# A mixture-of-experts stage on one core: where a place's sums are halved, when its result is added, and how short chunks are turned

## The chip, the cores and the metric

The kernel runs on one core of a Trainium2 chip. The metric is the device time of one execution in microseconds. It computes a two-layer trunk on 256 context and 256 latent tokens of width 1024, all in fp32. The change concerns the last stage of the second layer, the experts, which takes from about 900 us to the end.

## The reference, cut to what matters

```
def swiglu(h, wg, wu, wd):
    return (jax.nn.silu(h @ wg) * (h @ wu)) @ wd

def moe_ffn(h, w_r, wg, wu, wd):          # h: 256 x 1024, 8 experts, hidden width 2816
    logits = (h @ w_r).astype(jnp.float32)
    top_v, top_i = lax.top_k(logits, 2)
    gates = jax.nn.softmax(top_v, axis=-1)
    combine = jnp.sum(jax.nn.one_hot(top_i, 8) * gates[..., None], axis=-2)
    out = jnp.zeros_like(h)
    for e in range(8):
        out = out + combine[..., e:e + 1] * swiglu(h, wg[e], wu[e], wd[e])
    return out
# in the last layer: x = x + mod[5] * moe_ffn(...)
```

## The kernel before

After routing, the eight experts are put in order of their token counts into eight places (expert 0 is always place 7). A place has a fixed number of slots, `CAPS`: 160, 128, 128, 64, 64, 64, 32, 32. Places 0, 1 and 2 are wide: 128 slots, their weights split into a high and a low fp32r half (`whi` by a ScalarE copy, `wlo` by a VectorE subtraction, lines 275 and 276) and multiplied in three products. Place 0's slots beyond 128 are a 32-slot rest, called `NE`, which uses place 0's weights again. The 64- and 32-slot places multiply plain fp32, with several column blocks of a weight side by side in the array (`tiled`, `tiled_up`).

An expert's hidden width is cut into 11 chunks of 256. A chunk needs three loads of 1 MB: two for gate and up (`gu`), one for down (`dn`). `rounds()` sets the order: 4 rounds with a chunk of place 7 each, then 11 rounds each for places 1, 0 and 2, with one chunk of a 64-slot place (3, then 4, then 5) in each and a 32-slot chunk (places 7 and 6) in 6, 6 and 4 of them, then two rounds with a chunk of place 6. A round of `experts()` (line 1605) does: the wide chunk's gate products; the down product of the wide chunk of the round before (`down`, accumulating in two banks `py` over the 11 chunks); for place 0 the rest's gate (`gux`) and down (`down_rest`, `pyx`); the 32-slot and then the 64-slot chunk's gate and the down products of the round before (`down_small`, accumulating in the one bank `pys` or `pyx` of that slot count). Then the round's results are turned, so that the hidden width lies on the partitions: `turn` for the narrow ones, side by side in one bank `mTx`, and two transposes into a bank `mT` for the wide one. A 32-slot chunk lies in two parities on the partitions, which are added: `turn` multiplies it with `sel`, the sum of an identity and a swapped identity, so that one product turns and adds. `split` makes `mh` and `ml` of the wide chunk, `turned` makes silu(gate) times up (`silx`) of the narrow ones (line 1584). `mT`, `mTx`, `ohT`, `sc` and others share two banks.

When a place's last down product is issued, `finishes(p)` starts a chain (line 1747). Finishes go one after the other, whatever the place: each waits for the flag `finishing`. `finish` (line 1754) waits for the place's transposed one-hot matrix `ohT` (made by `onehot`, at most two at a time), multiplies the sums by the modulation row (`y`, lines 1766 and 1770), splits `y` into `yh` and `yl`, waits 3.0 us of the planner's clock, and then, per block of columns and half of the tokens, multiplies with `ohT` (a pair of `sc` products) and adds the gated result into `acc` (line 1780). A wide place does this in two halves of 512 columns, the second `y` made after the first half's pairs. The last place to finish stores `acc` block by block; that is place 6.

The order on TensorE and ScalarE in this stage is the order in which the program issues the instructions (`MSB = "pa"`); VectorE's and the load queue's order is chosen by the framework. The main order is `experts()`; chains like `finish`, `onehot` and `gather` are woven in at each of its `yield`s when the planner's clock `o.clk` has reached their due time. The clock advances by an estimated cost per product and, at `Weights.get`, to the modelled landing or split of a weight. All loads go through 12 raw buffers on one queue (SP).

```
RUNS = ((None, (4, 0)), (1, (6, 11)), (0, (6, 11)), (2, (4, 11)), (None, (2, 0)))
SMALL = ((7, 6), (3, 4, 5))
```

Of the kernel before, what the change touches and what calls it, by code (L numbers as in the profile page):

```python
# [18 lines left out]
P = 128  # L19
D = 1024  # L20
KB = D // P
# [4 lines left out]
NE = 8  # L26
# [3 lines left out]
EPS = 1e-6  # L30
# [179 lines left out]
def until(cond):  # L210
    while not cond():
        yield 0.5
# [128 lines left out]
class Net:  # L341
# [1150 lines left out]
    def onehot(self, p):  # L1492

        nc = self.nc
        yield from until(lambda: len(self.ohT) < 2)
        self.ohT[p] = None
        oh = self.mp.tile([P, 2, P], F32, tag="oh1", name="oh1", bufs=1)
        n = self.slots(p)
        for t in range(2):
            nc.vector.tensor_scalar(oh[:, t, :].rearrange("p (a b) -> p a b", b=n), self.c("iota", 0, n).unsqueeze(1).to_broadcast([P, P // n, n]),  # L1500
                                    self.pos0[:, t, 0:1] if p == NE - 1 else self.pos[:, t, p:p + 1], None, op0=ALU.is_equal)
        yield 1.5
        pt = self.bank("ohT")
        for t in range(2):
            self.tp(pt[:, P * t:P * t + P], oh[:, t, :])
        ohT = self.mp.tile([P, 2, P], F32R, tag="ohT", name="ohT", bufs=2)
# [5 lines left out]
    YB, YH = 1, 1  # L1512
    NRAW, MKRAW = 4, 5
    MPRAW, HL_B, LAG, NS = 3, 2, 6.0, 2
    PIECE, LANDS, SPLIT = 2.45, 4.8, 1.15
# [57 lines left out]
        self.nc.scalar.activation(v, ps[:, :256], AF.Copy)  # L1573
        return v

    def turn(self, pt, at, v, m):
        for j in range(2):
            b = v[:, P * j:P * j + P]
            if m == 32:
                self.mm(pt[:, at + 64 * j:at + 64 * j + 64], b, self.sel, True, True)  # L1580
            else:
                self.tp(pt[:, at + P * j:at + P * j + P], b)

    def turned(self, pt, at, m):

        src = pt[:, at:at + 4 * m].rearrange("p (j g s) -> p j g s", j=2, g=2)
        s = self.mp.tile([P, 2, m], F32, tag=f"silx{m}", name="silx", bufs=5 if m == 32 else 4)
        self.act_fn(s, src[:, :, 0, :], AF.Silu)
        self.nc.vector.tensor_tensor(s, s, src[:, :, 1, :], op=ALU.mult)
        return s  # L1590

    def experts(self):
# [8 lines left out]
        self.sel = self.mp.tile([P, 64], F32, name="sel", bufs=1)  # L1601
        nc.vector.tensor_tensor(self.sel, self.c("ident", 0, 64), self.c("swap", 0, 64), op=ALU.add)
        o.spawn(self.gather(0), 2)
        pw, pn = None, []
        for w, ns in self.rounds() + [(None, [])]:
# [5 lines left out]
            if w:  # L1611
                p, c = w
                x = self.xe[p]
# [39 lines left out]
            mids = []  # L1653
# [37 lines left out]
            at = 0  # L1691
            for p, c, m, v in mids:
                mx = self.turned(pt, at, m)
                at += 4 * m
                if p == NE:
                    pw[4] = mx
                else:
                    pn.append((p, c, mx))
            yield

    def down(self, p, c, mh, ml):
        a, z = c == 0, c == NCH - 1
        if a:
            self.py[p] = [self.pp.tile([P, 512], F32, tag="py", name="py", bufs=2) for _ in range(2)]
        w = self.w.get(("dn", p, c))
        for j in range(2):
            js = slice(P * j, P * j + P)
            for i, (u, v) in enumerate(((mh, w[0]), (ml, w[0]), (mh, w[1]))):
                for n in range(2):
                    ws = slice(D * j + 512 * n, D * j + 512 * n + 512)  # L1710
                    self.mm(self.py[p][n], u[:, js], v[:, ws], a and j == 0 and i == 0, z and j == 1 and i == 2)
        if c == NCH - 2 and p:
            self.o.spawn(self.onehot(p), 1)
        if z and p:
            self.o.spawn(self.finishes(p), 1)
        return w

    def down_rest(self, w, c, mx):
# [11 lines left out]
            self.o.spawn(self.onehot(0), 1)  # L1730
            self.o.spawn(self.onehot(NE), 1)
        if c == NCH - 1:
            self.o.spawn(self.finishes(0), 1)

    def down_small(self, p, c, mx):
        if c == 0:
# [5 lines left out]
        if c == NCH - 2:  # L1742
            self.o.spawn(self.onehot(p), 1)
        if c == NCH - 1:
            self.o.spawn(self.finishes(p), 1)

    def finishes(self, p):
        yield from until(lambda: not self.finishing)
        self.finishing = True
        for q in (p, NE) if p == 0 else (p,):  # L1750
            yield from self.finish(q)
        self.finishing = False

    def finish(self, p):

        nc = self.nc
        m = self.slots(p)
        parts = P // m
        w = 512 if m > 32 else 256
        yield from until(lambda: self.ohT.get(p) is not None)  # L1760
        ohT = self.ohT[p]
        for n in range(2 if m == P else 1):
            yh, yl = (self.mp.tile([P, 512], F32R, tag=nm, name=nm, bufs=self.YH) for nm in ("yh", "yl"))
# [9 lines left out]
            for g in (n,) if m == P else range(parts):  # L1773
                cs = slice(w * g, w * g + w)
                rows = slice(m * g, m * g + m) if parts > 1 else slice(0, P)
                for t in range(2):
                    pz = self.bank("sc")
                    for i, v in enumerate((yh, yl)):
                        self.mm(pz[:, :w], ohT[rows, t, :], v[rows, :w], i == 0, i == 1)
                    nc.vector.scalar_tensor_tensor(self.acc[:, t, cs], pz[:, :w], self.gate[:, t, p:p + 1], self.acc[:, t, cs],  # L1780
                                                   op0=ALU.mult, op1=ALU.add)
                    if self.ndone == NE:
                        nc.sync.dma_start(self.out[P * t:P * t + P, cs], self.acc[:, t, cs])
                    yield 1.0
        del self.ohT[p]
        self.ndone += 1

    def overflow(self):

# [85 lines left out]
    def run(self):  # L1875
# [7 lines left out]
        with tc.tile_pool(name="keep", bufs=1) as keep, ExitStack() as self.pools, ExitStack() as self.kax, tc.tile_pool(name="sm", bufs=2) as self.sp, \  # L1883
                tc.tile_pool(name="w", bufs=2) as self.wp:
            self.const = keep.tile([P, NKEEP], F32, name="const")
            self.params = keep.tile([P, NPARAM], F32, name="params")
            self.csil = keep.tile([P, KB, 38], F32, name="csil")
            self.eps = keep.tile([P, 1], F32, name="eps")
            self.modT = [keep.tile([P, 48, 2], F32, name=f"modT{l}") for l in range(2)]
            self.wr = keep.tile([P, KB, NE], F32, name="wr")  # L1890
            self.acoef = keep.tile([P, 16], F32, name="acoef")
            self.nsink = keep.tile([P, 16], F32, name="nsink")
            nc.scalar.dma_start(self.csil, d["cT"])
            self.act_fn(self.csil, self.csil, AF.Silu)
            nc.scalar.dma_start(self.params, d["params"])
            nc.scalar.dma_start(self.const[:, :2 * P], d["consts"][:, :2 * P])
            nc.vector.memset(self.eps, EPS)
            self.act_fn(self.acoef, self.par("a_log"), AF.Exp)
            nc.vector.tensor_scalar(self.acoef, self.acoef, -1.0, None, op0=ALU.mult)
            nc.vector.tensor_scalar(self.nsink, self.par("sink"), -1.0, None, op0=ALU.mult)  # L1900
            self.nb, self.nc_banks = 4, 3
            self.w = Weights(self, self.plan(), self.nraw, self.nhi)
            with tc.tile_pool(name="psA", bufs=4, space=PSUM) as self.pp, tc.tile_pool(name="g", bufs=self.ng) as self.gp:
                self.ka = self.kax.enter_context(tc.tile_pool(name="keepA", bufs=1))
                self.gb = self.kax.enter_context(tc.tile_pool(name="act", bufs=2 * KB))
                self.xpp = self.kax.enter_context(tc.tile_pool(name="xp", bufs=2))
                self.xT = [self.G(name=f"xT{k}") for k in range(KB)]
# [37 lines left out]
```

## Time and profile before

| | |
|---|---|
| three timed runs | 1581.52, 1585.33, 1587.26 us (median 1585.33) |
| the profiled execution | 1583.83 us; its span on the core 1582.1 us; granted TensorE clock 0.978 |
| TensorE busy | 1500.2 us (95%) |
| VectorE, ScalarE, GpSimd busy | 821.2, 666.7, 102.6 us |
| HBM read | 393.47 MB, of it 264 expert loads of 1 MB |

A row of the profile is a group of instructions with its busy time, or, in a timeline, one instruction or a run of like ones with its start and duration; in brackets stands how long the engine sat idle before it and what released it. PE is TensorE's products, PEld its weight loads, DVE VectorE, ACT ScalarE. A DMA share near 1 means that the 16 DMA engines moved packets all the time. A matmul's record overlaps its neighbours, so the spacing of starts, not the duration, is the price of one in a stream.

### The profile page before, as it was taken

How to read it: one execution, taken by the hardware profiler on the slowest of the kernel's cores; microseconds unless marked ns; L12 is line 12 of the kernel's file. 1: busy time of each engine (PE TensorE's matmuls, PEld its weight loads, DVE VectorE, ACT ScalarE, POOL GpSimd, SP SyncE). 2: the span in 40 equal slices, each digit the busy share in tenths (PEclk: the TensorE clock that was granted, in tenths of full speed). 3: DMA queues.
4: the chain of work that ended last, by engine and by line, in shares of the span. 5: the costliest groups of instructions: out<-in, count | busy, mean ns of one | idle time of the engine just before them, and what ended most of it. 6: DMA issues, size and time to landing. Idle time of an engine off the chain costs nothing. (4 is left out here: it accounts for less than half of the span.)

```text
span 1582.1 us, 23498 instructions
## 1 busy us (share of the span) xinstructions
PE 1500.2 (95%) x9302; PEld 1081.1 (68%) x9303; DVE 821.2 (52%) x1481; ACT 666.7 (42%) x1189; POOL 102.6 (6%) x135
## 2 busy tenths in 40 slices
PE   5999998899999999999999899999999999999997
PEld 1766675787887787878757776666566666656654
DVE  2687568543232333378774344544465444654545
ACT  3566644443222312266455354444343443433441
POOL 1200123210000000030300000000000000000000
PEclk9999999999999999999999899999999999999998
DMA  9422055333323323333164499999998999999994
GB/s 372 152 106 107 28 211 202 133 133 112 129 91 149 133 107 113 112 141 142 56 267 181 152 418 419 419 419 420 418 390 358 371 413 417 419 402 407 419 420 158
DMA packets 57715, 396.10 MB, mean 250 GB/s; under 512 B 6528, under 2 KB 8576, under 8 KB 10496
## 3 DMA queue, kind: packets, MB, share of 16 engines
q1 hardware_dynamic: 56016, 392.03, 62.2%
q10 hardware_dynamic: 1584, 2.52, 0.4%
q8 instruction: 75, 1.23, 0.3%
q14 instruction: 40, 0.33, 0.1%
HBM read 393.47 MB, written 1.05 MB: 249 GB/s over the span
## 5 line engine op out<-in xcount | busy, mean ns | idle before, releaser
L276 DVE TENSOR_TENSOR wlo<-wraw,whi 128x1024 fp32r<-128x1024 f32 (+2 forms) x318 | 377.0, 1222 | 161.2 <-ACT whi L275 155.9
L275 ACT ACTIVATE whi<-wraw 128x1024 fp32r<-128x1024 f32 (+2 forms) x318 | 320.0, 1047 | 148.5 <-PE fd L374 57.9
L374 PE MATMUL gu<-whi,xw 128*128 128x512 f32 x528 | 169.1, 401 | 4.2 <-ACT whi L275 4.2
L374 PE MATMUL gu<-wraw,xs 128*64 128x256 f32 (+1 forms) x1760 | 166.2, 386 | 0.5 <-ACT xs L1484 0.5
L374 PEld LDWEIGHTS gu<-wraw,xs 128*64 128x64 f32 (+1 forms) x1760 | 94.4, 127 | 64.3 <-issue 14.6
L374 PEld LDWEIGHTS gu<-whi,xw 128*128 128x128 f32 x528 | 96.9, 190 | 24.5 <-ACT whi L275 6.1
L374 PE MATMUL gu<-wlo,xw 128*128 128x512 f32 x264 | 104.9, 397 | 3.5 <-DVE wlo L276 3.5
L1162 DVE TENSOR_TENSOR fsil<-fsil,fu 128x512 f32<-128x512 f32 x22 | 15.1, 688 | 153.5 <-PE fu L374 118.2
L374 PE MATMUL pys<-wraw,silx 128*32 128x256 f32 (+1 forms) x616 | 87.6, 480 | 6.8 <-DVE y L1770 4.1
L425 ACT ACTIVATE fsil<-fg 128x512 f32<-128x512 f32 x22 | 13.1, 598 | 174.3 <-PE fg L374 174.3
L1573 ACT ACTIVATE mid<-gu 128x256 f32<-128x256 f32 x55 | 21.0, 382 | 137.1 <-PE gu L374 137.1
L374 PE MATMUL fg<-ahi,whi 128*128 128x512 f32 (+1 forms) x192 | 72.3, 377 | 0.0
L374 PE MATMUL fg<-alo,whi 128*128 128x512 f32 (+1 forms) x192 | 71.6, 373 | 0.2 <-POOL alo L523 0.2
L374 PE MATMUL fg<-ahi,wlo 128*128 128x512 f32 (+1 forms) x192 | 71.4, 372 | 0.0
L374 PE MATMUL fu<-alo,whi 128*128 128x512 f32 (+1 forms) x192 | 71.4, 372 | 0.0
L374 PE MATMUL fu<-ahi,wlo 128*128 128x512 f32 (+1 forms) x192 | 71.3, 372 | 0.0
L374 PE MATMUL fu<-ahi,whi 128*128 128x512 f32 (+1 forms) x192 | 71.3, 372 | 0.0
L374 PE MATMUL fd<-mhi,whi 128*128 128x512 f32 (+1 forms) x188 | 70.7, 376 | 0.0
L374 PE MATMUL fd<-mlo,whi 128*128 128x512 f32 (+1 forms) x188 | 70.6, 375 | 0.0
L374 PE MATMUL fd<-mhi,wlo 128*128 128x512 f32 (+1 forms) x188 | 70.6, 375 | 0.0
L374 PE MATMUL modp<-wraw,csil 128*32 128x512 f32 x384 | 56.7, 628 | 12.0 <-ACT csil L425 6.9
L374 PEld LDWEIGHTS gu<-wlo,xw 128*128 128x128 f32 x264 | 49.9, 189 | 18.3 <-DVE wlo L276 7.4
(342 smaller groups left out, 2831.8 us busy)
## 6 DMA issues: line engine op xcount, KB each, us to landing
wraw<-in_moe_dram SPq DMA_DIRECT2D x264, 1024.0 KB, 12.6
wraw<-in_wmod_dram SPq DMA_DIRECT2D x48, 1024.0 KB, 6.4
wraw<-in_fgu_dram SPq DMA_DIRECT2D x22, 1024.0 KB, 4.8
wraw<-in_win_dram SPq DMA_DIRECT2D x16, 1024.0 KB, 4.9
wraw<-in_wout_dram SPq DMA_DIRECT2D x8, 1024.0 KB, 6.2
wraw<-in_fdn_dram SPq DMA_DIRECT2D x8, 1024.0 KB, 6.2
wraw<-in_fdn_dram SPq DMA_DIRECT2D x4, 768.0 KB, 4.9
wraw<-in_wgd_dram SPq DMA_DIRECT2D x2, 1056.0 KB, 4.9
```

Of the source, the lines that this page charges most:

```text
L275: nc.scalar.activation(hi[:, cs], t[:, cs], AF.Copy)
L276: nc.vector.tensor_tensor(lo[:, cs], t[:, cs], hi[:, cs].bitcast(F32), op=ALU.subtract)
L374: self.nc.tensor.matmul(out, l, r, start=start, stop=stop)
L425: self.last_act = self.nc.scalar.activation(out, in_, func, **kw)
L1162: self.nc.vector.tensor_tensor(s, s, pu, op=ALU.mult)
L1573: self.nc.scalar.activation(v, ps[:, :256], AF.Copy)
```

## The change

A place's `y`, `yh` and `yl` are made by a new function `halves`, which `finished` runs at once when the place's last down product has been issued. A wide place's four halves of 512 columns lie in a buffer of the gathered tokens (`xw`). The chain that is left, `finish`, waits 3.0 us from there, or from the end of the modelled splits, and does the pairs. There is a flag for wide and one for narrow places, so one finish of either kind can be under way; a third `ohT` buffer is added. The finish of `NE` follows place 0's as a narrow one. The place that stores is named (`self.last`, place 6), and its pairs wait until all others are issued.

`turn` transposes every chunk plainly. A turned 32-slot chunk has 256 columns; `turned` copies the first parity of each half to SBUF on ScalarE and adds the second on VectorE (`sum32`) before silu and multiplication. The wide chunk is turned as the last of the round's jobs, and two jobs share a bank. Constants that only the first phase reads move from the pool `keep` into that phase's pool.

```diff
 def onehot(self, p):
-        yield from until(lambda: len(self.ohT) < 2)
+        yield from until(lambda: len(self.ohT) < 3)
...
-    def turn(self, pt, at, v, m):
+    def turn(self, pt, at, v):
         for j in range(2):
-            b = v[:, P * j:P * j + P]
-            if m == 32:
-                self.mm(pt[:, at + 64 * j:at + 64 * j + 64], b, self.sel, True, True)
-            else:
-                self.tp(pt[:, at + P * j:at + P * j + P], b)
+            self.tp(pt[:, at + P * j:at + P * j + P], v[:, P * j:P * j + P])
 
     def turned(self, pt, at, m):
-        src = pt[:, at:at + 4 * m].rearrange("p (j g s) -> p j g s", j=2, g=2)
+        src = pt[:, at:at + 256]
+        if m == 32:
+            v = src.rearrange("p (j r c) -> p j r c", j=2, r=2)
+            src = self.mp.tile([P, 2, 64], F32, tag="sum32", name="sum32", bufs=2)
+            self.nc.scalar.activation(src, v[:, :, 0, :], AF.Copy)
+            self.nc.vector.tensor_tensor(src, src, v[:, :, 1, :], op=ALU.add)
+            src = src.rearrange("p j (g s) -> p j g s", g=2)
+        else:
+            src = src.rearrange("p (j g s) -> p j g s", j=2, g=2)
...
-            if mids:
-                pt, at = self.bank("mTx"), 0
-                for *_, m, v in mids:
-                    self.turn(pt, at, v, m)
-                    at += 4 * m
+            jobs = [[x, x[3]] for x in mids] + ([[None, sil]] if w else [])
+            for i, x in enumerate(jobs):
+                if i % 2 == 0:
+                    pt = self.bank("mT" if i + 1 == len(jobs) else "mTx")
+                self.turn(pt, 256 * (i % 2), x[1])
+                x[1] = pt
             pw = None
             if w:
-                pm = self.bank("mT")
-                for j in range(2):
-                    self.tp(pm[:, P * j:P * j + P], sil[:, P * j:P * j + P])
+                at = 256 * ((len(jobs) - 1) % 2)
...
-                self.split(mh, ml, pm[:, :256])
+                self.split(mh, ml, jobs[-1][1][:, at:at + 256])
...
-    def finishes(self, p):
-        yield from until(lambda: not self.finishing)
-        self.finishing = True
-        for q in (p, NE) if p == 0 else (p,):
-            yield from self.finish(q)
-        self.finishing = False
...
+    def halves(self, p):
...
+        if m == P:
+            f = self.mp.tile([P, 2, KB, P], F32R, tag="xw", name="fin", bufs=2).rearrange("p a k s -> p (a k s)")
+            ys = [(f[:, 1024 * n:1024 * n + 512], f[:, 1024 * n + 512:1024 * n + 1024]) for n in range(2)]
+        else:
+            ys = [tuple(self.mp.tile([P, 512], F32R, tag=nm, name=nm, bufs=1) for nm in ("yh", "yl"))]
+        for n, (yh, yl) in enumerate(ys):
             y = self.mp.tile([P, 512], F32, tag="xsum", name="y", bufs=self.YB)
...
             self.split(yh[:, :w], yl[:, :w], y[:, :w])
-            yield 3.0
...
+        return ys
+
+    def finishes(self, p):
+        yield from self.finish(p, self.begin(p))
+        if p == 0:
+            yield from until(lambda: not self.finishing[False])
+            yield from self.finish(NE, self.begin(NE))
+
+    def begin(self, p):
+        self.finishing[self.wide(p)] = True
+        return self.halves(p)
+
+    def finished(self, p):
+        self.o.wait(lambda: not self.finishing[self.wide(p)])
+        self.o.spawn(self.finishes(p), 1)
+        self.o.poll()
+
+    def finish(self, p, ys):
...
+        yield max(3.0, self.w.splits - self.o.clk + 3.0)
+        yield from until(lambda: self.ohT.get(p) is not None)
+        ohT = self.ohT[p]
+        if p == self.last:
+            yield from until(lambda: self.ndone == NE)
...
```

## Rows read from the trace of the kernel before

**Rows 1.** Stretches: from:to and length, busy us (instructions) by engine, TensorE clock, DMA share, GB/s.

```profile
910.00:1150.00 240.00, 228.90 (x1560) 153.42 (x1553) 114.43 (x151) 109.93 (x182) 0.00 (x0) 0.99 1.01 419
1150.00:1300.00 150.00, 148.84 (x1192) 99.07 (x1190) 74.97 (x107) 62.99 (x107) 0.00 (x0) 1.00 0.94 381
1370.00:1460.00 90.00, 85.63 (x504) 55.41 (x506) 51.78 (x71) 34.74 (x53) 0.00 (x0) 0.96 1.00 406
```

**Rows 2.** Weight loads issued from 1100 to 1120, then from 1540: issue to landing.

```profile
DMA to landing us min/median/max: 19.8/19.8/19.9
...
L240 SPq DMA_DIRECT2D wraw<-in_moe_dram x1: 337/337/337, 1540.3 to 1540.3; - x1
DMA to landing us min/median/max: 16.3/16.3/16.3
```

**Rows 3.** Timeline of the tail: start, us, instruction, count, idle before and releaser.

```profile
1561.05 1.07 PE L374 MATMUL pys<-wraw,silx 128*32 128x256 f32 x16 [0.67 <-DVE silx L1589]
...
1569.00 1.29 DVE L1770 TENSOR_TENSOR y<-pys,mod5row 32x256 f32<-32x256 f32 x3
...
1570.41 0.42 ACT L437 ACTIVATE yh<-y 128x256 fp32r<-128x256 f32 x1 [5.92 <-DVE y L1770]
...
1570.88 0.57 PE L374 MATMUL sc<-yh,ohT 32*128 32x256 f32 x1 [2.68 <-ACT yh L437]
```

**Rows 4.** Timeline, turns at the end of a round of place 0.

```profile
1167.30 1.10 PE L374 MATMUL mTx<-sel,mid 128*128 128x64 f32 x8
...
1168.24 0.39 PE L379 MATMUL mTx<-const,mid 128*128 128x128 f32 x2
...
1168.46 0.38 PE L379 MATMUL mT<-const,sil 128*128 128x128 f32 x2
```

**Rows 5.** Groups of the expert phase: shapes, count, busy us, mean ns, idle before.

```profile
L374 PE MATMUL mTx<-sel,mid 128*128 128x64 f32 x132 | 20.2, 283 | 0.5 <-ACT mid L1573 0.5
...
L1780 DVE SCALAR_TENSOR_TENSOR acc<-sc,gate,acc 128x512 f32<-128x512 f32 x24 | 17.8, 750 | 28.0 <-PE sc L374 27.7
...
L1589 DVE TENSOR_TENSOR silx<-silx,mTx 128x128 f32<-128x128 f32 x33 | 9.3, 282 | 6.9 <-ACT silx L425 6.9
...
L425 ACT ACTIVATE silx<-mTx 128x128 f32<-128x128 f32 x33 | 9.1, 275 | 11.8 <-DVE silx L1589 11.8
...
L437 ACT ACTIVATE yh<-y 128x512 fp32r<-128x512 f32 x9 | 5.6, 625 | 9.1 <-DVE y L1766 5.4 <-PE sc L374 3.7
...
L1766 DVE TENSOR_TENSOR y<-py,mod5row 128x512 f32<-128x512 f32 x6 | 4.2, 692 | 4.1 <-PE py L374 3.9
```

**Rows 6.** Timeline, ScalarE and VectorE after the turns of two rounds.

```profile
1169.88 0.22 ACT L425 ACTIVATE silx<-mTx 128x64 f32<-128x64 f32 x1 [0.50 <-DVE silx L1589]
...
1171.47 2.01 ACT L275 ACTIVATE whi<-wraw 128x1024 fp32r<-128x1024 f32 x2 [0.80 <-PE gu L374]
...
1369.47 0.38 ACT L437 ACTIVATE mh<-mT 128x256 fp32r<-128x256 f32 x1 [3.13 <-PE mT L379]
...
1372.26 0.41 DVE L438 TENSOR_TENSOR ml<-mT,mh 128x256 fp32r<-128x256 f32 x1
```

**Rows 7.** Timeline around the first products of place 5, then two stretches.

```profile
1365.55 1.94 PE L374 MATMUL pys<-wraw,silx 128*64 128x512 f32 x8
...
1381.05 1.95 PE L374 MATMUL gu<-wraw,xs 128*64 128x256 f32 x16
...
1386.37 0.69 DVE L1770 TENSOR_TENSOR y<-pys,mod5row 64x512 f32<-64x512 f32 x1
...
1387.12 3.68 PE L374 MATMUL pys<-wraw,silx 128*64 128x512 f32 x8 [4.12 <-DVE y L1770]
...
1390.73 0.69 PE L379 MATMUL mTx<-const,mid 128*128 128x128 f32 x2
...
1380.00:1390.00 10.00, 5.88 (x32) 2.13 (x26) 5.86 (x7) 1.75 (x3) 0.00 (x0) 0.77 1.01 419
1390.00:1400.00 10.00, 10.00 (x41) 7.30 (x40) 4.91 (x10) 4.16 (x7) 0.00 (x0) 0.89 1.01 418
```

More of the change, by code (lines that the diff above doesn't have):

```diff
@@ L1511 @@
     SU = 4.0
-    YB, YH = 1, 1
+    YB = 1
     NRAW, MKRAW = 4, 5
@@ L1598, in experts @@
         self.xe, self.ohT, self.py = {}, {}, {}
-        self.finishing = False
+        self.finishing = [False, False]
         self.ndone = 0
-        self.sel = self.mp.tile([P, 64], F32, name="sel", bufs=1)
-        nc.vector.tensor_tensor(self.sel, self.c("ident", 0, 64), self.c("swap", 0, 64), op=ALU.add)
+        self.last = self.steps()[-1][1]
         o.spawn(self.gather(0), 2)
@@ L1714, in down @@
         if z and p:
-            self.o.spawn(self.finishes(p), 1)
+            self.finished(p)
         return w
@@ L1732, in down_rest @@
         if c == NCH - 1:
-            self.o.spawn(self.finishes(0), 1)
+            self.finished(0)
     def down_small(self, p, c, mx):
@@ L1744, in down_small @@
         if c == NCH - 1:
-            self.o.spawn(self.finishes(p), 1)
-    def finishes(self, p):
-        yield from until(lambda: not self.finishing)
-        self.finishing = True
-        for q in (p, NE) if p == 0 else (p,):
-            yield from self.finish(q)
[L1752 to L1757, printed above, removed]
+            self.finished(p)
+    def halves(self, p):
+        nc, m = self.nc, self.slots(p)
         parts = P // m
         w = 512 if m > 32 else 256
[L1760 to L1763, printed above, removed]
+        if m == P:
[4 more added lines that the diff above has]
+        for n, (yh, yl) in enumerate(ys):
             y = self.mp.tile([P, 512], F32, tag="xsum", name="y", bufs=self.YB)
@@ L1771, in finish @@
             self.split(yh[:, :w], yl[:, :w], y[:, :w])
-            yield 3.0
[L1773 to L1784, printed above, removed]
+        return ys
@@ new lines, in finishes @@
+    def finishes(self, p):
[11 more added lines that the diff above has]
+    def finish(self, p, ys):
+        nc = self.nc
+        m = self.slots(p)
+        parts = P // m
+        w = 512 if m > 32 else 256
+        wide = m == P
+        yield max(3.0, self.w.splits - self.o.clk + 3.0)
[3 more added lines that the diff above has]
+            yield from until(lambda: self.ndone == NE)
+        for g in range(D // w):
+            cs = slice(w * g, w * g + w)
+            rows = slice(0, P) if wide else slice(m * g, m * g + m)
+            for t in range(2):
+                pz = self.bank("sc")
+                for i, v in enumerate(ys[g if wide else 0]):
+                    self.mm(pz[:, :w], ohT[rows, t, :], v[rows, :w], i == 0, i == 1)
+                nc.vector.scalar_tensor_tensor(self.acc[:, t, cs], pz[:, :w], self.gate[:, t, p:p + 1], self.acc[:, t, cs],
+                                               op0=ALU.mult, op1=ALU.add)
+                if p == self.last:
+                    nc.sync.dma_start(self.out[P * t:P * t + P, cs], self.acc[:, t, cs])
+                yield 1.0
@@ L1785, in finish @@
         del self.ohT[p]
         self.ndone += 1
+        self.finishing[wide] = False
     def overflow(self):
@@ L1886, in run @@
             self.params = keep.tile([P, NPARAM], F32, name="params")
-            self.csil = keep.tile([P, KB, 38], F32, name="csil")
             self.eps = keep.tile([P, 1], F32, name="eps")
-            self.modT = [keep.tile([P, 48, 2], F32, name=f"modT{l}") for l in range(2)]
+            self.modT = [None, keep.tile([P, 48, 2], F32, name="modT1")]
             self.wr = keep.tile([P, KB, NE], F32, name="wr")
[L1891 to L1900, printed above, removed]
             self.nb, self.nc_banks = 4, 3
@@ L1904, in run @@
                 self.ka = self.kax.enter_context(tc.tile_pool(name="keepA", bufs=1))
+                self.csil = self.ka.tile([P, KB, 38], F32, name="csil")
+                self.modT[0] = self.ka.tile([P, 48, 2], F32, name="modT0")
+                self.acoef = self.ka.tile([P, 16], F32, name="acoef")
+                self.nsink = self.ka.tile([P, 16], F32, name="nsink")
+                nc.scalar.dma_start(self.csil, d["cT"])
+                self.act_fn(self.csil, self.csil, AF.Silu)
+                nc.scalar.dma_start(self.params, d["params"])
+                nc.scalar.dma_start(self.const[:, :2 * P], d["consts"][:, :2 * P])
+                nc.vector.memset(self.eps, EPS)
+                self.act_fn(self.acoef, self.par("a_log"), AF.Exp)
+                nc.vector.tensor_scalar(self.acoef, self.acoef, -1.0, None, op0=ALU.mult)
+                nc.vector.tensor_scalar(self.nsink, self.par("sink"), -1.0, None, op0=ALU.mult)
                 self.gb = self.kax.enter_context(tc.tile_pool(name="act", bufs=2 * KB))
```

11 lines of the change are left out of this document (6 added, 5 removed).

## The prediction

> **What bounds the kernel now.** I read the stretches of the expert phase first [rows 1]. From 910 to 1150 us the DMA engines move 419 GB/s at a share of 1.01: transfers set the pace there. From 1150 to 1300 they move 381 GB/s while TensorE is busy 148.84 of 150 us; these are the rounds of place 0. From 1370 to 1460 they move 406 GB/s. Against 419 the two later stretches lose 150 x (1 - 381/419) = 13.6 us and 90 x (1 - 406/419) = 2.8 us of transfer time. All expert weights pass through 12 raw buffers, so the transfers pause where TensorE is late in freeing them.
>
> The time from issue to landing [rows 2] says how near TensorE is to the transfers. At 1100 to 1120 it is 19.8 us, about eight pieces of 2.5 us (1.05 MB at 419 GB/s) queued ahead: TensorE uses what lands. The last piece is issued at 1540.3 and lands 16.3 us later, at 1556.6; its product, the last `pys` [rows 3], starts at 1561.05. So at the end TensorE lies 4.4 us behind the transfers, and from about 1150 on it is TensorE's own order of work that carries the time, with the transfers close beneath. The end then has a tail: from the end of that `pys` at 1562.1 to the end of the span at 1582.1.
>
> **Part 1: 32-slot chunks turned plainly.** Before, two chunks are turned by eight matmul records with the `sel` matrix, from 1167.30 to 1168.24, 0.47 us a chunk; the plain turn of a 64-slot chunk, two records, takes from 1168.24 to 1168.46, 0.22 us [rows 4]. After, each 32-slot chunk costs the plain price: 0.25 us less on TensorE. 132 records [rows 5] at four a chunk are 33 chunks: 22 of places 7 and 6 and 11 of the rest `NE`. Place 0's rounds hold 6 + 11 of them, place 2's hold 4: 17 x 0.25 = 4.3 us and 4 x 0.25 = 1.0 us. The 10 chunks ahead of place 0's rounds lie where transfers set the pace and are worth nothing; two of the last rounds belong to the tail.
>
> In exchange each chunk gets a ScalarE copy and a VectorE add of 128x128. The nearest rows are the `silx` steps of that shape that read the same bank: 0.275 and 0.282 us [rows 5]; I take these, with nothing and twice that as ends. 17 x 0.56 = 9.5 us of busy time on two engines that are busy 63 and 75 of the 150 us [rows 1], so beside TensorE's products. On ScalarE's order little is added: today the second `silx` of a bank waits 0.50 us for VectorE's multiply out of it [rows 6]; after, the multiply reads SBUF, and the add takes that wait's place. The first reader of the turned chunk is the next round's down product, behind a whole wide gate product.
>
> **Part 2: halves at the last down product.** A 64-slot place's sums lie in a bank of which there is one. Place 4's were read by `y` only behind the finishes of place 0 and of `NE`, the second half at 1386.37; place 5's first down product waited for it 4.12 us on TensorE [rows 7]. Behind that wait the granted clock is 0.77 and 0.89 in two windows of 10 us [rows 7], part of the time at 1.2 instead of 2.4 GHz: the eight `pys` records take 3.68 us against 1.94 at full clock, 1.74 us more. The turns behind them (0.69 against 0.39 for the same two records [rows 4, 7]) and the first gate products run at the low level too; an estimate of 0.6 us from these rows. Together 6.4 us. After, `y` follows the last down product at once, a whole round ahead of the next place's, so this wait goes; what is late next there is the landing of the weights.
>
> The halves cost what they cost before: for a wide place two `y` of 0.69, two `yh` of 0.63 us and two `yl`, taken like `y` [rows 5]. What is new is their place in ScalarE's order, which is fixed with TensorE's: ScalarE stands at `yh` until the product and `y` have ended, and the copies of `mid` and the splits (`whi`) behind it wait. One buffer for `y` makes a wide place's six steps a chain of about 4 us. The narrow products that follow last longer than this (a 64-slot gate takes two groups of 1.95 us and its down product 1.94 [rows 7]), and the next split weights are wanted a round later, so I count nothing; without that cover up to 4 us for each of the two wide places with wide rounds behind them.
>
> **Part 3: finishes side by side, the tail.** Today, after the last `pys`, TensorE and VectorE still do two pairs of place 2 and all four of place 5, then place 6's `y` (three of four parts at 1569.00), `yh` at 1570.41, and place 6's first pair at 1570.88 [rows 3]: 8.8 us after 1562.1. After, places 2 and 5 finish in turn from the narrow rounds on; by the planner's clock (3.0 from the halves, 1.0 between pairs) half of their eight pairs stand ahead of that `pys` and about four behind. Behind it then come four adds into `acc` of 0.75 us [rows 5], four `y` of 0.43, one `yh` of 0.42 [rows 3] and some 0.7 us of gaps: 3.0 + 1.7 + 0.4 + 0.7 = 5.8, so 3.0 us less. The last chunk's turn is on the path: -0.25 for the plain turn, +0.56 for copy and add and 0.1 for two hand-overs, 0.4 us later. Tail: -2.6 us. With all pairs still behind it is 0, with none -6.0. Place 6's own eight pairs and the stores are untouched.
>
> **Part 4: the rest.** Constants that only the first phase reads move to its pool, `sel` goes, and a third one-hot buffer comes. No engine's order in the first phase changes by this; other addresses can make a load wait for another tile. I count nothing, and a microsecond either way.
>
> **Sum.** TensorE's path: 4.3 + 1.0 + 6.4 = 11.7 us. The transfers cap it: of 13.6 us lost, 4.3 return in place 0's rounds, the 2.8 us go, and of the 4.4 us between last landing and last product some 3.4 can be caught up: 10.5 us. I take 9.5, one microsecond for new small waits. With the tail 12.1 us. The profiled execution took 1583.83 us (span 1582.1 and 1.7 around it): 1571.7. Its time is 1.5 us below the median of the runs, 1585.33; from that it is 1573.2. I say 1573.
>
> **Rivals.** *The transfers keep the time.* Only the 2.8 us of the later stretch return and the tail's 2.6, because the additions on ScalarE eat what TensorE saves in place 0's rounds: 5 us, 1580. For it: TensorE is only 4.4 us behind the landings at the end. Against: the transfers, not TensorE, have the gaps [rows 1].
>
> *ScalarE stands behind VectorE.* In 18 of the 33 wide rounds (those with an even number of turned chunks: 5 of place 1, 6 of place 0, 7 of place 2) the wide chunk and the 64-slot chunk now share a bank; before they never did. Two readers of one bank come one after the other here, as the 0.50 us show [rows 6]. So ScalarE's `silx` of the 64-slot chunk will wait for VectorE's `ml`, and `ml` can stand behind splits: `mh` ended at 1369.85 and `ml` began only at 1372.26, 2.4 us later [rows 6]. The next `whi` waits behind it; it had 0.80 us to spare [rows 6]. So up to 1.6 us late in a round, in the 13 rounds of places 0 and 2: 21 us, against 12 gained: +9, 1593. It decides from about 0.9 us a round on. Against it: other `ml` follow `mh` quickly, and the gate products ahead give more cover than that 0.80.
> The Trainium skill, PSUM — Partial Sum Buffer, section on bank collisions, says the same more strictly: no two engines may touch one bank in the same quadrant at once, ScalarE and VectorE reading included, and the compiler puts a dependency between them. By that rule the sharing costs in every such round. The trace agrees that the wait is there; that it reaches TensorE, no row shows.
>
> *The tail does not shorten.* VectorE has to fit eight adds of 0.75 us, the halves and the new adds into the last 12 us; then the sum is 9.5 alone, 1576, still on the forecast's side.
>
> **Chances.** Forecast, the tail's rival included: 0.66. Transfers keep the time: 0.22. ScalarE behind VectorE: 0.09. Something small either way, as loads moved by addresses: 0.03. About 0.5%, 7.9 us, is what a measurement can tell from no change. So faster by more (under 1577.4) 0.66, within it 0.24, slower 0.10. The range: the tail at its best and the full 11.7 give 17.7 us, 1567.6, and 2 us below that for waits that I don't see, 1565.5; upward it takes in the first rival and no change, 1585. The forecast's own range is 1566 to 1577.
>
> **What would show it.** Right: no wait of `pys` for `y` and a clock of 1.00 near 1380; the transfers from 1150 to 1300 above 381 GB/s; two records a turned 32-slot chunk; place 6's first `sc` pair some 6 us after the last `pys`. Wrong: ScalarE idle in front of `silx` with VectorE's `ml` as releaser and TensorE's wide products waiting for `whi` behind it; `yh` holding ScalarE through a wide gate product; or the transfers from 1150 to 1300 at 381 GB/s again.

## The result, and the profile after

The changed kernel takes 1592.49 us (median of 16 runs, 1587.36 to 1595.54) against 1583.39 (16 runs, 1579.17 to 1587.40): 1.0055 times as long, 95% interval 1.0042 to 1.0067. It is slower by 9.1 us, outside the forecast's range. The profiled execution has a span of 1590.9 us against 1582.1 and a granted clock of 0.972 against 0.978; TensorE is busy 1501.1 us, VectorE 830.7, ScalarE 674.7.

Where the span grew, by events that both traces have:

| | before | after | |
|---|---|---|---|
| last norm of the first phase starts (`rs_v`, line 403) | 889.3 | 895.0 | +5.7 |
| first down product of place 1 starts (`py`) | 945.4 | 952.5 | +7.1 |
| transfer time lost, 1120 to 1300: 180 x (1 - rate/419) | 387 GB/s: 13.7 | 373 GB/s: 19.8 | +6.1 |
| the same, 1380 to 1460: 80 x (1 - rate/419) | 404 GB/s: 2.9 | 419 GB/s: 0 | -2.9 |
| last weight lands | 1556.6 | 1567.1 | +10.5 |
| end | 1582.1 | 1590.9 | +8.8 |

In what follows the start of that norm stands for the end of the first phase. 7.1 + 6.1 - 2.9 = 10.3 of the 10.5 us. The transfers of the expert phase set the end in both kernels; they begin later, lose more around place 0, and only the later loss is gone. The stretches of the changed kernel, in the columns of [rows 1] (from:to, length, busy us by engine, clock, DMA share, GB/s):

```profile
910.00:1150.00 240.00, 226.20 (x1586) 148.91 (x1580) 110.65 (x154) 112.86 (x193) 0.00 (x0) 0.98 1.00 415
1150.00:1300.00 150.00, 143.21 (x1142) 94.56 (x1138) 80.04 (x118) 62.63 (x112) 0.00 (x0) 0.98 0.89 363
1370.00:1460.00 90.00, 86.38 (x509) 53.91 (x508) 55.94 (x75) 38.36 (x57) 0.00 (x0) 1.00 1.01 419
1380.00:1390.00 10.00, 7.34 (x29) 4.61 (x27) 9.86 (x14) 4.41 (x8) 0.00 (x0) 1.00 1.01 419
1390.00:1400.00 10.00, 10.00 (x57) 5.78 (x58) 5.18 (x9) 4.19 (x5) 0.00 (x0) 1.00 1.01 419
```

Against [rows 1, 7]: from 1370 on the loss is gone and the clock at 1380 to 1400 is 1.00, as forecast. From 1150 to 1300 the rate is 363, lower than the 381 before, and TensorE, which was busy nearly all of it, is idle for 6.8 us. TensorE's waits of the expert phase (waiting product, releaser, total us, times, longest) name the place:

```profile
PE gu L374 <- DVE wlo L276: 6.5, 15, 0.9
PE sc L374 <- DVE ml L438: 5.5, 1, 5.5
PE gu L374 <- ACT whi L275: 5.5, 4, 2.6
PE pys L374 <- DVE silx L1593: 4.5, 3, 2.8
```

The wait of `pys` for `y` (4.12 us in [rows 7]) is not among them; one wait of 5.5 us for `ml` is new. In the timeline (start, us, instruction, count, idle before and releaser) it stands at the end of place 1:

```profile
1152.90 0.63 PE L379 MATMUL mTx<-const,mid 128*128 128x128 f32 x4 [0.94 <-DVE acc L1806]
1153.36 0.38 PE L379 MATMUL mT<-const,sil 128*128 128x128 f32 x2
...
1153.51 4.63 DVE L276 TENSOR_TENSOR wlo<-wraw,whi 128x1024 fp32r<-128x1024 f32 x4
...
1158.77 0.42 DVE L438 TENSOR_TENSOR ml<-mT,mh 128x256 fp32r<-128x256 f32 x1
...
1159.25 1.22 PE L374 MATMUL sc<-fin,ohT 128*128 128x512 f32 x2 [5.51 <-DVE ml L438]
1160.27 1.05 PE L374 MATMUL gu<-whi,xw 128*128 128x512 f32 x2
...
1159.42 0.26 ACT L425 ACTIVATE silx<-sum 128x64 f32<-128x64 f32 x1 [4.84 <-DVE sum L1587]
...
1164.88 2.01 ACT L275 ACTIVATE whi<-wraw 128x1024 fp32r<-128x1024 f32 x2 [5.03 <-issue]
```

Both shared banks are full of turned chunks. A finish product (`sc`) stands next in TensorE's order and needs one of them; VectorE does four splits before `ml`, which reads the bank. Behind the idle time the clock is 0.87 and 0.79, the gate products take 1.05 us a pair instead of 0.62 or 0.63, and the transfers pause because no raw buffer comes free (from 1150 to 1180 the load queue's longest wait is 18.0 us, for a product of TensorE, `gux`):

```profile
1150.00:1160.00 10.00, 3.56 (x18) 1.73 (x13) 8.46 (x13) 1.49 (x5) 0.00 (x0) 0.87 1.02 419
1160.00:1170.00 10.00, 10.00 (x33) 7.00 (x32) 4.86 (x7) 2.39 (x3) 0.00 (x0) 0.79 0.35 143
1170.00:1180.00 10.00, 10.00 (x112) 5.84 (x112) 5.18 (x7) 4.55 (x6) 0.00 (x0) 1.00 0.49 188
```

And the tail, to be read against [rows 3]:

```profile
1573.01 1.22 PE L374 MATMUL pys<-wraw,silx 128*32 128x256 f32 x16 [1.30 <-DVE silx L1593]
...
1578.49 0.43 DVE L1767 TENSOR_TENSOR y<-pys,mod5row 32x256 f32<-32x256 f32 x1
...
1579.02 0.42 ACT L437 ACTIVATE yh<-y 128x256 fp32r<-128x256 f32 x1 [2.60 <-DVE y L1767]
...
1579.49 0.57 PE L374 MATMUL sc<-yh,ohT 32*128 32x256 f32 x1 [1.80 <-ACT yh L437]
```

Place 6's first pair comes 5.3 us after the end of the last `pys` (8.8 before). But that `pys` starts 5.9 us after the last landing, where it was 4.5.

### The profile page after: what moved, and what is told of

Its sections match the earlier page's. It is cut to its first block, busy times and chain, and to the rows that moved or that the text cites. A ratio compares the mean times of both kernels' runs of the same rounds, so it can differ in the third digit from the quotient of the medians.

```text
span 1590.9 us, 23437 instructions
## 1 busy us (share of the span) xinstructions
PE 1501.1 (94%) x9236; PEld 1071.9 (67%) x9237; DVE 830.7 (52%) x1513; ACT 674.7 (42%) x1222; POOL 103.9 (7%) x135
## 3 DMA queue, kind: packets, MB, share of 16 engines
HBM read 393.47 MB, written 1.05 MB: 248 GB/s over the span
```

## The experiments

Ratios are to runs of the kernel before on the same chip; its medians there were 1583.3 to 1583.6 us. Brackets are 95% intervals. The diffs are cut; `...` stands for what is left out, and remarks behind `#` do not stand in the kernels.

### The first phase: an offset in SBUF

In the dense stage the gate and up products of the changed kernel follow each other every 0.2333 us:

```profile
462.25 0.39 PE L374 MATMUL fg<-ahi,whi 128*128 128x512 f32 x1
462.49 0.39 PE L374 MATMUL fg<-alo,whi 128*128 128x512 f32 x1
462.72 0.39 PE L374 MATMUL fg<-ahi,wlo 128*128 128x512 f32 x1
462.95 0.39 PE L374 MATMUL fu<-ahi,whi 128*128 128x512 f32 x1
```

Before it was 0.2267; the down products `fd` keep 0.2267 in both, at a clock of 1.00 in both. Theory A: the moved constants (1728 bytes a partition) shifted the split weights but not the activations, which lie behind the pool that received the constants, so that the two operands of a product no longer begin at the same offset within 256 bytes. Theory B: the first 100 us or the order.

```diff
+                self.pada = self.ka.tile([P, 16], F32, name="pada")   # a_pad64: behind nsink; b_pad64: head of that pool, kernel before
...
+                self.pada = self.ka.tile([P, 32], F32, name="pada")   # b_pad128: the same place, kernel before
...
+            self.padk = keep.tile([P, 48], F32, name="padk")          # a_both: with pada, behind wr
```

**a_pad64.**

> The changed kernel with one unused tile of 64 bytes per partition put behind the moved constants in the first phase's pool; nothing else. It moves the normed activations (ahi, alo) by 64 bytes, so that they and the split weights (whi, wlo) again begin at the same offset within 256 bytes, as before the change (in the changed kernel they stand 192 bytes apart). Theory A, the place of the operands in SBUF: the gate and up products of the dense stage go back from a spacing of 0.2333 us to 0.2267 us, the last norm of the first phase ends near 889 us instead of 895, and the time falls by 4 to 7 us, to about 1586 to 1588. Theory B, the first phase is late because of its first 100 us (granted clock 0.80 against 0.90 in the first 50 us) or of a changed order: spacing and time stay as in the changed kernel, 1592 within 2 us.

Measured 1587.12 us, 1.0025 [1.0010, 1.0039]: 5.4 us under the changed kernel, the intervals apart. The first phase ends at 889.0, and the spacing is back:

```profile
457.23 0.39 PE L374 MATMUL fg<-ahi,whi 128*128 128x512 f32 x1
457.46 0.39 PE L374 MATMUL fg<-alo,whi 128*128 128x512 f32 x1
457.69 0.39 PE L374 MATMUL fg<-ahi,wlo 128*128 128x512 f32 x1
457.91 0.39 PE L374 MATMUL fu<-ahi,whi 128*128 128x512 f32 x1
```

64 unused bytes take back more than half of the loss. Theory B is out.

**b_const**, the prediction's last part alone, on the kernel before:

```diff
-            self.csil = keep.tile([P, KB, 38], F32, name="csil")
...
+                self.csil = self.ka.tile([P, KB, 38], F32, name="csil")
```

> The kernel before with the move of the constants alone (csil, one modT, acoef and nsink from the lasting pool into the first phase's pool), that is the prediction's last part by itself. The prediction put it at 0 with 1 us either way: 1582.4 to 1584.4. Theory A: the first phase ends some 5.7 us later and the time is 1587 to 1591, which is more than half of what the whole change lost. Theory B: no change if the late start was chance; if it came with this move, the lag shows in the first 100 us and not in the spacing of the products.

Measured 1587.71, 1.0034 [1.0016, 1.0053]; spacing 0.2333; the first phase ends at 897.7. The step that was costed at nothing costs 4.2 us without the rest. The size is rough: the twelve runs lie in two groups, seven from 1585.1 to 1587.8 and five from 1591.6 to 1592.7, and the trace is of the slowest.

**b_pad64.**

> The kernel before with one unused tile of 64 bytes per partition at the head of the first phase's pool; nothing else. It puts ahi and alo 64 bytes away from the split weights in their offset within 256 bytes. Theory A (place of the operands): the dense stage's gate and up products go from 0.2267 to about 0.2333 us, the first phase ends 4 to 7 us later and the time is 1587 to 1591. If only some offsets cost (192 bytes apart but not 64), or under theory B (the start, or the order): 1583.4 within 2 us.

Measured 1583.04, 1.0002 [0.9986, 1.0018]; mean spacing 0.2290, the first phase ends at 887.8. A miss: at this offset the products slow down by a third as much, an estimated 2 us, and the time doesn't show it.

**b_pad128**, one run.

> The kernel before with an unused tile of 128 bytes per partition at the head of the first phase's pool: ahi and alo begin 128 bytes off from the split weights in their offset within 256 bytes. Read for the spacing of the dense stage's gate and up products alone (0.2267 us at no offset, 0.229 at 64, 0.2333 at 192). If the offset counts by its distance, 128 gives the most, 0.233 or more; if what counts is whether the operands lie within the same 128 bytes or so, 0.2267 again.

1594.92 us; spacing 0.2333, the first phase ends at 897.8. The spacing is that at 192.

**a_both.**

> The changed kernel with the 64 bytes in the first phase's pool and 192 bytes more in the pool that stands below the weights, so that the raw expert weights in all 12 buffers and the narrow tokens (xs) also begin at the same offset within 256 bytes as before (in the changed kernel the five buffers on the right side stand 192 bytes apart from them). Theory A: the first phase as with the 64 bytes alone; if the place of the operands also counts for the narrow products, places 1 and 0, which TensorE keeps, go some us faster than there (200 of 528 gate products of the 64-slot places are apart): 1580 to 1585. If the narrow products don't mind: the same as with the 64 bytes alone, within 1.5 us. Theory B: 1592.

Measured 1587.48, 1.0033 [1.0017, 1.0049]: no better than the 64 bytes alone. No cost of the narrow products' offset shows. What is left, some 4 us, is in the expert phase. The kernels below are built on this one, so that all operands lie as before.

### The expert phase: finishes against turns

**finish_only**, the turns and the end of a round from the kernel before:

```diff
-                self.turn(pt, 256 * (i % 2), x[1])
...
+                    self.turn(pt, at, v, m)
...
```

> The changed kernel with both paddings (all operands at their old offsets), and in it the turns of the kernel before (sel, the wide chunk in a bank of its own). What is left of the change is the halves at the last down product and the finishes side by side. Its TensorE order has a finish product of place 1 right behind the turns, as the changed kernel has. Theory S (the time still lost, some 4 us with the paddings, comes from that product: it waits 5.5 us for a bank that VectorE's ml frees behind four splits, the weights' buffers come free late and the transfers fall to 166 GB/s for 20 us): the stall is here too, 1584 to 1589. Theory V (the loss comes from the copies and additions of the plain turns and the shared banks): no loss is left, and the wait for y is gone: 1578 to 1582.

Measured 1584.61, 1.0015 [1.0000, 1.0030]. The stall is there (`sc` waits 5.3 us for `ml`), and the transfers lose 180 x (1 - 369/419) = 21.5 us from 1120 to 1300. So the stall belongs to the finishes; the `y` wait's gain and a shorter tail pay for most of it.

**turns_only**, the finishes and two `ohT` buffers from the kernel before:

```diff
-            self.finished(p)
+            self.o.spawn(self.finishes(p), 1)
...
```

> The changed kernel with both paddings, and in it the finishes of the kernel before (one after the other, the halves inside the chain); left of the change are the plain turns with the sum on ScalarE and VectorE and the shared banks. The finish products of place 1 come behind half of the next gate product, as before. Theory S: no stall; the turns give what the prediction's first part says or less, 1577 to 1583. Theory V: the loss is here, 1585 to 1589, with ScalarE idle ahead of silx and whi late.

Measured 1586.80, 1.0022 [1.0006, 1.0038]. No stall, and still slower, which theory S had not expected: the turns have a price of their own, so both theories held a part.

**hold.** One product pair moved:

```diff
+            self.hold = bool(w)              # at the turns; False again after half of the next gate product
...
+                yield from until(lambda: not self.hold)
                 pz = self.bank("sc")
...
```

> The changed kernel with both paddings and one product pair moved: a flag keeps finish products out of the stretch between a wide round's turns and the first half of the next gate product. TensorE's order differs from the padded kernel in one place only, where place 1's last finish product stands behind the first twelve gate products of place 0's first round and not ahead of them. Theory S: the wait of 5.5 us goes or falls under 1.5, the 20 us with 166 GB/s too, and the time falls from 1587.5 to between 1579 and 1583, under the kernel before. Theory V: within 2 us of 1587.5.

Measured 1582.33, 1.0004 [0.9987, 1.0022]: 5.2 us under the padded kernel. The wait is down to 1.9 us, where under 1.5 was expected; the pair now stands behind twelve gate products:

```profile
1146.44 0.38 PE L379 MATMUL mT<-const,sil 128*128 128x128 f32 x2
...
1152.33 0.73 PE L374 MATMUL sc<-fin,ohT 128*128 128x512 f32 x2 [1.90 <-DVE ml L438]
```

**f_hold**, finish_only with the lines of hold.

> Finishes of the change, turns of the kernel before, both paddings, and the flag that keeps finish products out of the stretch from a wide round's turns to the first half of the next gate product. Theory S (the stall at place 1's end is what the finishes cost, the y wait at place 2 is what they give): the wait of 5.3 us and the loss behind it go, the transfers lose 8 to 13 us from 1120 to 1300 (21 with the stall, 13.6 before) and about nothing from 1380 to 1460, and the time is 1577 to 1581, 3 to 7 us under the kernel before. Rival: the halves on ScalarE's fixed order cost by themselves; then 1583 or more.

Measured 1579.54, 0.9981 [0.9965, 0.9996], in the expected band. From 1120 to 1300 the transfers lose 180 x (1 - 382/419) = 15.9 us, somewhat more than expected; the rest of the wait and one of 2.8 us for a bank (`mT` <- `acc`) are still there. finish_only and f_hold differ by that one pair, and by 5.1 us.

For the turns I compared the time between down products, from the starts of each round's first `py`:

| | before | turns_only | copy_max | turns_place0 |
|---|---|---|---|---|
| place 1's rounds, first to eleventh `py` | 184.3 | 187.6 | 187.4 | 184.3 |
| issue to landing at 1120 to 1140, median | 16.2 | 10.0 | 10.7 | 14.3 |
| place 0's rounds, ten | 205.5 | 202.1 | 205.5 | 202.1 |
| a round of place 2 with a 32-slot chunk, the sixth | 18.5 | 20.1 | 20.3 | 18.4 |
| granted clock in it | 1.00 | 0.92 | 0.92 | 1.00 |
| 22nd to 33rd `py`, place 2's rounds | 190.7 | 194.3 | 192.5 | 190.6 |

In place 0 the turns save 3.4 us for 16 chunks, somewhat less than the forecast's 0.25 us a chunk. In place 1 TensorE becomes 3.3 us later, in rounds that the transfers pace, and the pieces queued ahead melt: from 1120 to 1140 it is 10 us from issue to landing instead of 16. Place 2 loses 3.6 us more, and there the traces show how. In the sixth round TensorE waits 1.16 us for `whi` where it waited 0.91, the clock falls behind the wait, and the round grows by 1.6 us while the transfers stay at full rate. Before, then turns_only:

```profile
1464.76 0.73 PE L374 MATMUL gu<-whi,xw 128*128 128x512 f32 x2 [0.91 <-ACT whi L275]
...
1466.35 0.63 PE L374 MATMUL gu<-whi,xw 128*128 128x512 f32 x2
...
1460.00:1480.00 20.00, 18.44 (x111) 11.02 (x108) 11.23 (x13) 10.35 (x15) 0.00 (x0) 1.00 1.01 419
```

```profile
1466.47 0.73 PE L374 MATMUL gu<-whi,xw 128*128 128x512 f32 x2 [1.16 <-ACT whi L275]
...
1468.07 0.91 PE L374 MATMUL gu<-whi,xw 128*128 128x512 f32 x2
...
1460.00:1480.00 20.00, 18.20 (x102) 11.28 (x100) 10.94 (x13) 9.42 (x14) 0.00 (x0) 0.91 1.01 419
```

**turns_place0**, turns_only with both ways of turning:

```diff
+            if w and w[0] == 0:
...
+                    self.plain(pt, 256 * (i % 2), x[1])
...
+            else:
...
+                        self.turn(pt, at, v, m)
...
```

> Turns alone again (finishes as before, both paddings), but plain only in the rounds of place 0; the rounds of places 7, 1 and 2 use sel as before. Theory L (in rounds that the transfers pace, a plain turn puts the copy and the wait for VectorE's addition ahead of the next whi on ScalarE; the later TensorE there eats the pieces that are queued ahead, and place 0 begins with 10 to 12 us from issue to landing where it had 16): without plain turns ahead of place 0 the entry is as before and place 0's rounds still take 0.22 to 0.45 us less each: the transfers lose 9 to 11 us from 1120 to 1300, and the time is 1578.5 to 1581.5. Rival (the additions cost in place 0 as much as the turns save): no better than with plain turns everywhere, 1584 to 1588.

Measured 1581.47, 0.9985 [0.9970, 0.9999], apart from turns_only. The same turns, left out of the rounds of all places but 0, gain instead of lose.

**copy_max**: TensorE's order of the kernel before, with the two steps added:

```diff
+        if m == 32:
+            v = self.mp.tile([P, 2, 2, 32], F32, tag="sum32", name="sum32", bufs=2)
+            self.nc.scalar.activation(v, src, AF.Copy)
+            self.nc.vector.tensor_tensor(v, v, src, op=ALU.max)
+            src = v
```

> The kernel before (its turns with sel, its banks, its finishes, TensorE's order unchanged), the constants moved with both paddings, and for each turned 32-slot chunk the two added steps alone: a ScalarE copy out of the bank and a VectorE step on it (a maximum with the same values, which changes nothing) ahead of silx. TensorE saves nothing. Theory L (the copy and ScalarE's wait for VectorE stand ahead of the next whi): the rounds that carry a 32-slot chunk under places 1 and 2 grow as with the plain turns (15.83 to 16.3, 18.46 to 19 or 20), place 0's rounds grow or stay and don't shrink, place 0 is entered with fewer than 14 us from issue to landing, and the time is 1585 to 1590. Rival (what costs is that the wide and a narrow chunk share a bank, so that ScalarE stands behind ml): banks are as before here, so the rounds are those of the kernel before and the time is 1583 within 2 us.

Measured 1588.56, 1.0032 [1.0017, 1.0047]. The two steps alone lose 5 us. The expected growth from 15.83 did not come, though; those rounds (the third, fifth and ninth of place 1) stay at 15.85, 15.86 and 16.90 here and are 16.35, 16.37 and 17.46 with the plain turns. They carry no 32-slot chunk: there the wide and the 64-slot chunk share a bank. ScalarE in such a round, before and then with turns_only:

```profile
972.95 0.38 ACT L437 ACTIVATE mh<-mT 128x256 fp32r<-128x256 f32 x1 [0.97 <-PE mT L379]
973.23 0.27 ACT L425 ACTIVATE silx<-mTx 128x128 f32<-128x128 f32 x1
973.39 3.19 ACT L275 ACTIVATE whi<-wraw 128x1024 fp32r<-128x1024 f32 x3
```

```profile
974.26 0.38 ACT L437 ACTIVATE mh<-mTx 128x256 fp32r<-128x256 f32 x1 [0.97 <-PE mTx L379]
975.13 0.28 ACT L425 ACTIVATE silx<-mTx 128x128 f32<-128x128 f32 x1 [0.49 <-DVE ml L438]
975.30 2.94 ACT L275 ACTIVATE whi<-wraw 128x1024 fp32r<-128x1024 f32 x3
```

`silx` waits 0.49 us for VectorE's `ml` on the same bank, `whi` starts 1.04 us after `mh` instead of 0.44, and a gate product behind it waits. That is the rival of the shared bank, at 0.5 us in each of three rounds. About half of what copy_max and turns_only lose in place 1, 1.6 and 1.5 us, is one round with the clock down. In copy_max 4.4 of the 4.9 us by which the time from the first to the 33rd `py` grows lie in three rounds whose clock is lower than before: that one, the seventh of place 1, then place 1's eleventh (0.86 against 0.93) and place 2's sixth. The seventh in copy_max, then before:

```profile
1034.00:1038.00 4.00, 3.35 (x10) 2.43 (x11) 3.75 (x5) 3.65 (x5) 0.00 (x0) 0.80 1.01 418
1038.00:1042.00 4.00, 4.00 (x34) 1.97 (x35) 1.53 (x2) 0.00 (x0) 0.00 (x0) 0.78 1.01 420
```

```profile
1034.00:1038.00 4.00, 3.54 (x20) 2.32 (x24) 3.75 (x5) 3.46 (x5) 0.00 (x0) 1.00 1.00 416
1038.00:1042.00 4.00, 4.00 (x48) 2.42 (x42) 1.34 (x2) 0.00 (x0) 0.00 (x0) 1.00 1.02 424
```

**f_hold_t0**, f_hold with the branch of turns_place0.

> All that should help put together: the change's finishes, the flag, both paddings, and plain turns in place 0's rounds alone. Theories S and L together: the gains add, 1574 to 1578, the time that the prediction gave to the change itself. If either falls, 1580 or more.

Measured 1578.84, 0.9973 [0.9957, 0.9989]: faster than both kernels, by 4.4 us than the one before. It is just above the expected band; from 1120 to 1300 it still loses 180 x (1 - 385/419) = 14.6 us, no less than before. It lies so close to f_hold that the turns' part of the gain is not shown by the times in this combination. The spans on the core say more: their medians are 1575.4 us here and 1577.8 in f_hold. Both kernels with two ways of turning spend more of their time outside the span (medians of 2.9 and 3.4 us, against 1.7 to 2.0 in the others), which hides part of the gain; why they do is open.

## Why the prediction was wrong

The medians add up: 5.0 us for the offset (1592.5 to 1587.5), 5.2 for the stall (to 1582.3) and 3.5 for the plain turns outside place 0 (to 1578.8). Without these three the change gains 4.4 us, not 12.1.

**Part 4, "I count nothing, and a microsecond either way", failed first.** I asked whether a load would wait for another tile, and not whether a product runs as fast at another address. a_pad64 and b_const measure it at 4 to 5.4 us. An estimate from the trace agrees: 960 gate and up products of 512 columns in the dense stage (160 of each of six kinds), 6.6 ns more for each, 6.3 us. Where the first phase ends differs by up to 6 us between traces that lie alike, so one trace alone proves little; but the three at 128 or 192 bytes end it at 895.0 to 897.8, all others at 885.6 to 891.8.

**Part 2, "so I count nothing" for the halves' new place.** The wait for `y` went as said, with the clock behind it, and the four rounds around it (22nd to 26th `py`) take 76.8 us instead of 79.9. The danger that I named, ScalarE held by `yh`, came in part, inside those 76.8 us: at 1383.19 ScalarE has been idle 5.57 us in front of `yh`, `mh` and the next `whi` stand behind it, and the gate products wait 1.12 us for `whi` and 0.87 for `wlo`:

```profile
1383.19 0.63 ACT L437 ACTIVATE yh<-y 128x512 fp32r<-128x512 f32 x1 [5.57 <-DVE y L1767]
...
1385.50 0.28 ACT L425 ACTIVATE silx<-mTx 128x128 f32<-128x128 f32 x1 [1.41 <-DVE ml L438]
...
1386.78 0.73 PE L374 MATMUL gu<-whi,xw 128*128 128x512 f32 x2 [1.12 <-ACT whi L275]
```

What cost more is an order effect: finish products fall due sooner, and one lands right behind the turns, when both shared banks are taken. I never asked which bank a finish product would find. finish_only, hold and f_hold show it: 5 us from one pair.

**Part 1, "worth nothing" for chunks where the transfers set the pace.** Place 0's saving is 3.4 us over ten rounds, 0.21 a chunk where I had 0.25. But outside place 0 the turns lose: what they add on ScalarE stands ahead of the next `whi`, TensorE waits longer for it (1.16 us against 0.91), and behind such waits the clock fell, which costs more than the wait. So the rounds paced by transfers gained nothing here, as I had said, but they lost. turns_place0 and copy_max show this from both sides. That the melted queue itself costs time is not shown: place 0's rounds take 205.5 us in copy_max, as before, though they begin with fewer pieces ahead. The changed kernel's own trace has less of it: place 1's rounds take 185.3 us, and the sixth of place 2 20.1 at a clock of 0.92. My sentence that the first reader of the turned chunk is far away was true and beside the point: what mattered was the split queued behind the added copy.

**Part 3, the tail.** Behind the last `pys` the forecast holds: 3.5 us less to place 6's first pair against 3.0. But the pairs moved to the front of that `pys` delay it, so that the 3.4 us of catching up did not come: from the last round's first `py` to that `pys` it is 16.9 us in f_hold and 13.7 before. In the changed kernel it starts 1.4 us later after the last landing. From last landing to end it is 25.5 us before, 23.8 after, 21.2 in f_hold and 24.2 in hold. The finishes alone bring 4.3 us, and the plain turns take 3.0 of them back where I had put 0.4: in hold the last `pys` waits 1.29 us for `silx`, in f_hold 0.57, and the next pair runs with the clock down. Hold, then f_hold:

```profile
1563.21 1.07 PE L374 MATMUL pys<-wraw,silx 128*32 128x256 f32 x16 [1.29 <-DVE silx L1593]
1564.22 0.79 PE L374 MATMUL sc<-yh,ohT 64*128 64x512 f32 x1
```

```profile
1561.59 1.07 PE L374 MATMUL pys<-wraw,silx 128*32 128x256 f32 x16 [0.57 <-DVE silx L1589]
1562.59 0.49 PE L374 MATMUL sc<-yh,ohT 64*128 64x512 f32 x1
```

**The rivals.** ScalarE behind VectorE had the right mechanism and the wrong place and price: 0.5 us in three rounds of place 1, once 1.41 us in front of `silx` at the start of place 2 (the rows of part 2, with TensorE waiting behind it), nothing visible in place 0, where I had put up to 1.6 a round. The Trainium skill, PSUM — Partial Sum Buffer, section on bank collisions, says that two engines are kept apart on one bank; the trace agrees, with the 0.49 us above. The rival's 1593 is close to the measured 1592.5 by chance. It had `ml` late behind splits, as in the stall, but with `whi` as what waits, not a product in need of the bank. None of my rivals had the stall as it came, or the offset.

Open is why the end of the first phase differs by up to 6 us between kernels that lie alike there (885.6 in copy_max, 891.8 in turns_place0), and why the clock falls in place 1's seventh round: TensorE's wait ahead of it is 1.67 us in copy_max and before, and the low stretch is in the traces of a_pad64, a_both, turns_only, hold and copy_max, not in that of the changed kernel.

## What to carry to other kernels

Moving a tile is not free until you have compared the spacing of the products that read what lies behind it. When a chain is released earlier, ask what it will need at its new place (here a bank) and who frees it. In a stretch that transfers pace, added work on an engine that feeds TensorE can still cost: compare TensorE's waits and the granted clock behind them, round by round.

## What the runs showed of the hardware

The spacing of fp32r products of 512 columns depended on where their operands begin within 256 bytes of SBUF, as the built programs place them. With the activation and the weight at the same offset it was 0.2267 us; with the activation 64 bytes on 0.2290; 128 bytes 0.2333; 192 bytes 0.2333, all at a clock of 1.00. The kernel before had all its fp32r products of 512 columns at the same offset. Why the offset matters is not shown. The Trainium skill, SBUF — State Buffer, section on operand start alignment, gives what starts are legal and says that its measurements timed nothing; these runs add the time.

TensorE's clock fell behind idle times of different lengths. Behind waits of 0.91 and 0.53 us it stayed at 1.00 (place 2's sixth round, before); with 1.16 in place of 0.91 it was 0.92 over the round, part of the time at 1.2 instead of 2.4 GHz (turns_only). Behind a wait of 1.67 us it stayed at 1.00 before and was 0.90 in copy_max (place 1's seventh round). So the wait's length alone did not decide it here.
